# Turning a table lookup's indices with one VectorE transpose in place of TensorE, in an embedding kernel

## The chip, the cores and the metric

One core of one Trainium2 chip. The metric is the device time of one execution in microseconds (us); the median of the runs is quoted. The experiments ran on three chips. The kernel before took 181.7 to 181.8 us on the first (called A here) and 176.1 to 176.2 us on the other two (B and C), so only runs of one chip are compared, or runs of B with runs of C, which agree within 0.1 us.

## The reference

```python
batch, seq_len, vocab_size, d_model = 32, 512, 50000, 512
token_embed = embedding_table[indices]            # indices: [32, 512]
return (token_embed + position_embed).astype(np.float32)   # [32, 512, 512]
```

16,384 rows of 2 KB are fetched, a position row is added to each, and 33.5 MB are written. The indices reach the core as 64-bit words; the low half of each is used.

## The kernel before

A sequence `b` lies on 128 partitions with 4 positions (`k`) on each. GpSimd issues 128 gathers; each takes one column of 128 indices and fetches 256 KB. VectorE adds the positions out of PSUM, ACT issues all other loads and all stores. For the first four sequences the indices are loaded in the layout that the gathers want, in small packets. The rest are loaded in rows, cast to float, turned by TensorE against an identity and cast back.

```python
with tc.tile_critical(sync_engine=nc.vector.engine, no_gpsimd_drain=True):
    nc.scalar.dma_start(out=idx0[:, 0, :], in_=idx_first[:, 0, :]).then_inc(s_first, 16)
    load_pos(0)                                   # half of the positions, 512 KB
    nc.scalar.dma_start(out=idx0[:, 1:, :], in_=idx_first[:, 1:, :]).then_inc(s_next, 16)
    nc.scalar.dma_start(out=idx_raw[:], in_=...).then_inc(s_raw, 16)      # 128 rows of 1 KB
    nc.scalar.wait_ge(s_pos[0], 16)
    load_pos(1)
    nc.gpsimd.affine_select(out=ident[:], ...)
    nc.gpsimd.wait_ge(s_first, 16)
    for g, (b, k) in enumerate(order):
        if g == half:       nc.gpsimd.wait_ge(s_next, 16)           # half is 2
        if g == FIRST * K:  nc.gpsimd.wait_ge(s_prep, 2 + K + J)    # 16: turned indices
        ...                                       # where = idx0[...] if b < FIRST else idx_t[...]
        nc.gpsimd.indirect_dma_start(out=slots[b % SLOTS][:, k, :], ...)
    # TensorE: 4 transposes; VectorE: 1 cast before them, 4 after, between its adds
    ...
tc.no_sync_barrier()
nc.scalar.wait_ge(s_rest, nc.scalar.to_reg(16 * rest))
```

## Time and profile before

| | before |
|---|---|
| time, median of 3 runs | 181.71 us (181.65 to 181.85) |
| span of the profiled run | 178.1 us |
| GpSimd | 133 instructions, 121.8 us busy |
| VectorE | 137 instructions, 91.4 us busy |
| TensorE | 4 transposes, 1.0 us busy |

Read the GpSimd row with care: 68% busy looks like slack, but each gather also has 0.30 us of "issue" before it, time in which the engine waits for nothing that the profile shows.

### The profile page before, as it was taken

The page shows a single profiled execution, that of the slowest core. Times are in us where ns is not written, and L with a number is a line of the kernel's source. Part 1 is how long each engine was busy: PE and PEld are TensorE (multiplying, and loading weights), DVE is VectorE, ACT ScalarE, POOL GpSimd, SP SyncE. Part 2 cuts the span into 40 slices and gives each one's busy share as a digit, 9 for nine tenths or more (in the row PEclk, how much of TensorE's full clock was granted, in tenths as well). Part 3 has the DMA queues.
Part 4 walks back from the last instruction along what each step waited for, and adds up shares of the span by engine and source line. Part 5 has one row for each costly group of instructions (what it writes and reads, how often), then busy time and mean ns, then how long its engine had stood idle before and what let it go on. Part 6 is the DMA issues. An engine that isn't in the chain of part 4 may idle for free.

```text
span 178.1 us, 415 instructions
## 1 busy us (share of the span) xinstructions
PE 1.0 (1%) x4; PEld 0.4 (0%) x4; DVE 91.4 (51%) x137; POOL 121.8 (68%) x133
## 2 busy tenths in 40 slices
PE   0000100000000000000000000000000000000000
PEld 0000000000000000000000000000000000000000
DVE  0445973455556555555556455555556555554510
POOL 3777777777777777777777777777777777774000
DMA  4899999999999999999999999999999999999960
GB/s 122 234 329 359 375 378 364 385 410 413 416 416 419 419 419 420 419 420 419 419 420 420 419 419 418 419 418 419 420 419 420 418 420 420 420 419 421 417 258 0
DMA packets 21011, 68.34 MB, mean 384 GB/s; under 512 B 3728, under 2 KB 3856, under 8 KB 21008
## 3 DMA queue, kind: packets, MB, share of 16 engines
q10 hardware_dynamic: 10768, 34.76, 48.6%
q0 software_dynamic: 10240, 33.56, 48.1%
q14 instruction: 3, 0.02, 0.0%
HBM read 34.75 MB, written 33.55 MB: 384 GB/s over the span
## 4 chain that ended last, share of the span: by engine, by line
POOL 65%; issue 23%; DMA 5%; DVE 2%; ACTq 0%; DVEq 0%
POOL slot L136 65%; DMA slot<-in_embedding_table_dram,idx_t 4%; DVE slot L171 2%; DMA idx<-in_indices_dram 1%; ACTq L211 0%; DVEq L101 0%
## 5 line engine op out<-in xcount | busy, mean ns | idle before, releaser
L136 POOL DMA_INDIRECT slot<-in_embedding_table_dram,idx_t x112 | 106.0, 946 | 34.1 <-issue 34.1
L171 DVE TENSOR_TENSOR slot<-slot,pos_ps 128x512 f32<-128x512 f32 x128 | 87.7, 687 | 73.8 <-issue 57.8
L136 POOL DMA_INDIRECT slot<-in_embedding_table_dram,idx x16 | 15.3, 958 | 6.0 <-issue 4.6
L166 DVE COPY pos_ps<-pos_sb 128x512 f32<-128x512 f32 x4 | 2.7, 685 | 4.9 <-DMA pos_sb<-in_position_embed_dram 4.9
L162 DVE CAST idx_t<-turned 32x128 int32<-32x128 f32 x4 | 1.1, 280 | 0.1
L149 PE MATMUL turned<-ident,idx_f 128*32 128x128 f32 x4 | 1.0, 413 | 17.6 <-issue 17.6
L118 POOL TENSOR_SCALAR_AFFINE_SELECT ident<-const-float32-1.0 128x128 f32<-128x128 f32 x1 | 0.3, 282 | 0.7 <-DVEq L101 0.7
L149 PEld LDWEIGHTS turned<-ident,idx_f 128*32 128x32 f32 x4 | 0.4, 131 | 17.7 <-issue 17.6
L200 POOL MEMSET const-float32-0.0<- 128x1 f32 x1 | 0.1, 99 | 0.3 <-issue 0.3
L156 DVE CAST idx_f<-idx_raw 128x128 f32<-128x128 int32 x1 | 0.2, 220 | 0.0
L200 POOL MEMSET const-uint8-127<- 128x1 uint8 x1 | 0.1, 116 | 0.0
L200 POOL MEMSET const-bfloat16-1.0<- 128x1 bf16 x1 | 0.1, 110 | 0.0
L200 POOL MEMSET const-float32-1.0<- 128x1 f32 x1 | 0.1, 102 | 0.0
## 6 DMA issues: line engine op xcount, KB each, us to landing
out_dram<-slot ACTq DMA_DIRECT2D x60, 512.0 KB
out_dram<-slot ACTq DMA_DIRECT2D x8, 256.0 KB
slot<-in_embedding_table_dram,idx_t POOLq DMA_INDIRECT x112
pos_sb<-in_position_embed_dram ACTq DMA_DIRECT2D x2, 512.0 KB, 4.7
slot<-in_embedding_table_dram,idx POOLq DMA_INDIRECT x16
idx_raw<-in_indices_dram ACTq DMA_DIRECT2D x1, 128.0 KB
idx<-in_indices_dram ACTq DMA_DIRECT2D x1, 4.0 KB, 1.6
idx<-in_indices_dram ACTq DMA_DIRECT2D x1, 12.0 KB
```

Of the source, the lines that this page charges most:

```text
L118: nc.gpsimd.affine_select(out=ident[:], in_=nc.const_aps.tensor(1.0, [P, P], f32), pattern=[[-1, P]], compare_op=mybir.AluOpType.is_equal, ...
L136: ins = nc.gpsimd.indirect_dma_start(out=slots[b % SLOTS][:, k, :], out_offset=None, in_=table, in_offset=bass.IndirectOffsetOnAxis(ap=whe ...
L149: nc.tensor.transpose(turned[:, k].rearrange("p b j -> p (b j)"), idx_f[:, :, k], ident[:]).then_inc(s_prep, 1)
L156: nc.vector.tensor_copy(out=idx_f[:].rearrange("r p k -> r (p k)"), in_=idx_raw[:, :, 0])._wait_ge(s_raw, 16).then_inc(s_prep, 1)
L162: nc.vector.tensor_copy(out=idx_t[j * Q : (j + 1) * Q, :, :], in_=turned[:, :, :, j]).then_inc(s_prep, 1)
L166: nc.vector.tensor_copy(out=pos_ps[:, k, :], in_=pos_sb[:, k, :])._wait_ge(s_pos[k // half], 16).then_inc(s_ps, 1)
L171: nc.vector.tensor_tensor(out=part, in0=part, in1=pos_ps[:, k, :], op=add)._wait_ge(s_gather[g % LANES], rounds(g)).then_inc(s_add, 1)
L200: nc = _bacc.Bacc("TRN2", target_bir_lowering=False, num_devices=1)
```

## The change

The intent is to take TensorE, the identity, the PSUM tile and five casts out of the index path. The row blocks are loaded with the 32 sequences on each quadrant of 32 partitions, in four loads, and one VectorE transpose of 128x128 words then yields the gathers' layout for all sequences: in this layout that means turning each square of 32x32 words where it lies. The small load for sequences 1 to 3 goes away, so everything from the third gather on waits for the transpose. GpSimd, not VectorE, gives the signal with which the section begins and ends.

```diff
-    with tc.tile_critical(sync_engine=nc.vector.engine, no_gpsimd_drain=True):
+    with tc.tile_critical(sync_engine=nc.gpsimd.engine, no_gpsimd_drain=True):
-        nc.scalar.dma_start(out=idx0[:, 0, :], in_=idx_first[:, 0, :]).then_inc(s_first, 16)
+        nc.scalar.dma_start(out=idx0[:, :], in_=idx_first).then_inc(s_first, 16)
         load_pos(0)
-        nc.scalar.dma_start(out=idx0[:, 1:, :], in_=idx_first[:, 1:, :]).then_inc(s_next, 16)
-        nc.scalar.dma_start(out=idx_raw[:], in_=...).then_inc(s_raw, 16)
+        for j in range(J):                                            # J is 4
+            nc.scalar.dma_start(
+                out=idx_raw[j * B : (j + 1) * B, :], in_=idx_rows[:, j, :]
+            ).then_inc(s_raw, 16)
         nc.scalar.wait_ge(s_pos[0], 16)
         load_pos(1)
-        nc.gpsimd.affine_select(out=ident[:], ...)
...
             if g == half:
-                nc.gpsimd.wait_ge(s_next, 16)
-            if g == FIRST * K:
-                nc.gpsimd.wait_ge(s_prep, 2 + K + J)
+                nc.gpsimd.wait_ge(s_idx, 1)
...
-        for k in range(K): nc.tensor.transpose(turned[:, k]..., idx_f[:, :, k], ident[:])
+        nc.vector.transpose(
+            out=idx_t[:],
+            in_=idx_raw[:].rearrange("r (q k w) -> r k q w", k=K, w=2)[:, :, :, 0],
+        )._wait_ge(s_raw, 16 * J).then_inc(s_idx, 1)
...                                               # (five casts between the adds: gone)
```

More of the change, by code (lines that the diff above doesn't have):

```diff
@@ L38 @@
     assert S == P * K and B == 32
-    assert V < (1 << 24), "an index passes through float32"
     J = P // Q
+    assert B == Q, "indices are turned in squares of 32"
     idx_words = indices.bitcast(i32)
-    idx_first = idx_words[0:FIRST].rearrange("b (p w) -> p b w", p=P)
-    idx_rows = idx_words.rearrange("b (j w) -> (b j) w", j=J)
+    idx_first = idx_words[0].rearrange("(p w) -> p w", p=P)
+    idx_rows = idx_words.rearrange("b (j w) -> b j w", j=J)
     out_rows = out.rearrange("b (p k) d -> b p k d", k=K)
@@ L57, in psum @@
         return ctx.enter_context(pool).tile(shape, dtype, name=name)
-    idx0 = sbuf("idx0", [P, FIRST, 2 * K], i32)
-    idx_raw = sbuf("idx_raw", [P, Q * K, 2], i32)
-    ident = sbuf("ident", [P, P], f32)
-    idx_f = sbuf("idx_f", [P, Q, K], f32)
+    idx0 = sbuf("idx0", [P, 2 * K], i32)
+    idx_raw = sbuf("idx_raw", [P, 2 * Q * K], i32)
     idx_t = sbuf("idx_t", [P, K, B], i32)
@@ L65 @@
     slots = [sbuf(f"slot{n}", [P, K, D], f32) for n in range(SLOTS)]
-    turned = psum("turned", [Q, K, B, J], f32)
     pos_ps = psum("pos_ps", [P, K, D], f32)
@@ L82 @@
     sem = tc.alloc_semaphore
-    s_first, s_next, s_raw = sem("s_first"), sem("s_next"), sem("s_raw")
+    s_first, s_raw, s_idx = sem("s_first"), sem("s_raw"), sem("s_idx")
     s_pos = [sem(f"s_pos{h}") for h in range(2)]
@@ L88 @@
     s_out, s_rest = sem("s_out"), sem("s_rest")
-    s_prep, s_ps, s_add = sem("s_prep"), sem("s_ps"), sem("s_add")
+    s_ps, s_add = sem("s_ps"), sem("s_add")
     def rounds(g):
@@ L99, in load_pos @@
         )
-    with tc.tile_critical(sync_engine=nc.vector.engine, no_gpsimd_drain=True):
-        nc.scalar.dma_start(out=idx0[:, 0, :], in_=idx_first[:, 0, :]).then_inc(
-            s_first, 16
-        )
+    with tc.tile_critical(sync_engine=nc.gpsimd.engine, no_gpsimd_drain=True):
+        nc.scalar.dma_start(out=idx0[:, :], in_=idx_first).then_inc(s_first, 16)
         load_pos(0)
-        nc.scalar.dma_start(out=idx0[:, 1:, :], in_=idx_first[:, 1:, :]).then_inc(
-            s_next, 16
-        )
-        nc.scalar.dma_start(
-            out=idx_raw[:], in_=idx_rows.rearrange("r (s w) -> r s w", w=2)
-        ).then_inc(s_raw, 16)
+        for j in range(J):
+            nc.scalar.dma_start(
+                out=idx_raw[j * B : (j + 1) * B, :], in_=idx_rows[:, j, :]
+            ).then_inc(s_raw, 16)
         nc.scalar.wait_ge(s_pos[0], 16)
         load_pos(1)
-        nc.gpsimd.affine_select(
-            out=ident[:], in_=nc.const_aps.tensor(1.0, [P, P], f32),
-            pattern=[[-1, P]], compare_op=mybir.AluOpType.is_equal, fill=0.0,
-            base=0, channel_multiplier=1,
-        ).then_inc(s_prep, 1)
         nc.gpsimd.wait_ge(s_first, 16)
@@ L131 @@
                 nc.gpsimd.wait_ge(s_out, 16 * done)
-            if b < FIRST:
-                where = idx0[:, b, 2 * k : 2 * k + 1]
+            if g < half:
+                where = idx0[:, 2 * k : 2 * k + 1]
             else:
@@ L144 @@
         nc.gpsimd.drain()
-        nc.tensor.wait_ge(s_prep, 2)
-        for k in range(K):
-            nc.tensor.transpose(
-                turned[:, k].rearrange("p b j -> p (b j)"), idx_f[:, :, k], ident[:]
-            ).then_inc(s_prep, 1)
-        for g, (b, k) in enumerate(order):
-            if g == 7:
-                nc.vector.tensor_copy(
-                    out=idx_f[:].rearrange("r p k -> r (p k)"), in_=idx_raw[:, :, 0]
-                )._wait_ge(s_raw, 16).then_inc(s_prep, 1)
-            if g == 9:
-                nc.vector.wait_ge(s_prep, 2 + K)
-                for j in range(J):
-                    nc.vector.tensor_copy(
-                        out=idx_t[j * Q : (j + 1) * Q, :, :], in_=turned[:, :, :, j]
-                    ).then_inc(s_prep, 1)
+        nc.vector.transpose(
+            out=idx_t[:],
+            in_=idx_raw[:].rearrange("r (q k w) -> r k q w", k=K, w=2)[:, :, :, 0],
+        )._wait_ge(s_raw, 16 * J).then_inc(s_idx, 1)
+        for g, (b, k) in enumerate(order):
             if b == 0:
```

## The prediction

> **What bounds the kernel now.** I read the page from the top down: the 40 slices, the chain that ended last, the groups, then the timeline of the first 25 us and of the end. The slices first:
>
> ```profile
> POOL 3777777777777777777777777777777777774000
> DMA  4899999999999999999999999999999999999960
> GB/s 122 234 329 359 375 378 364 385 410 413 416 416 419 419 419 420 419 420 419 419 420 420 419 419 418 419 418 419 420 419 420 418 420 420 420 419 421 417 258 0
> ```
>
> GpSimd shows an even 7 tenths up to slice 36, and the DMA engines are full. The chain and the groups say why GpSimd's 7 is in truth a full engine:
>
> ```profile
> POOL 65%; issue 23%; DMA 5%; DVE 2%; ACTq 0%; DVEq 0%
> L136 POOL DMA_INDIRECT slot<-in_embedding_table_dram,idx_t x112 | 106.0, 946 | 34.1 <-issue 34.1
> L171 DVE TENSOR_TENSOR slot<-slot,pos_ps 128x512 f32<-128x512 f32 x128 | 87.7, 687 | 73.8 <-issue 57.8
> L162 DVE CAST idx_t<-turned 32x128 int32<-32x128 f32 x4 | 1.1, 280 | 0.1
> L149 PE MATMUL turned<-ident,idx_f 128*32 128x128 f32 x4 | 1.0, 413 | 17.6 <-issue 17.6
> ```
>
> Each of 128 gathers takes 0.95 us of GpSimd and has 0.30 us of issue before it. The idle time is issue and no wait: all 34.1 us before the 112 gathers are "issue". So one gather starts every 1.25 us, and the chain is 88% GpSimd and issue. The last gather starts at 161.94 in the timeline of the end; the first at 2.89; 127 gaps of 1.25 us are 158.9, which with the 0.2 us extra of the first gap gives 159.05. That is the whole span but for a head of 2.89 us and a tail of 178.1 - 161.94 = 16.2 us. The head:
>
> ```profile
> 1.03 0.38 ACTq L104 DMA_DIRECT2D idx<-in_indices_dram  x1
> 1.18 0.28 POOL L118 TENSOR_SCALAR_AFFINE_SELECT ident<-const-float32-1.0 128x128 f32<-128x128 f32 x1 [0.67 <-DVEq L101]
> 1.44 0.45 ACTq L97 DMA_DIRECT2D pos_sb<-in_position_embed_dram  x1
> 1.93 0.46 ACTq L108 DMA_DIRECT2D idx<-in_indices_dram  x1
> 2.41 0.51 ACTq L111 DMA_DIRECT2D idx_raw<-in_indices_dram  x1
> 2.89 1.14 POOL L136 DMA_INDIRECT slot<-in_embedding_table_dram,idx  x1 [1.43 <-DMA idx<-in_indices_dram]
> 4.33 0.95 POOL L136 DMA_INDIRECT slot<-in_embedding_table_dram,idx  x1 [0.31 <-issue]
> 4.93 0.33 ACTq L97 DMA_DIRECT2D pos_sb<-in_position_embed_dram  x1
> 4.93 0.69 DVE L166 COPY pos_ps<-pos_sb 128x512 f32<-128x512 f32 x1 [4.93 <-DMA pos_sb<-in_position_embed_dram]
> 5.59 0.95 POOL L136 DMA_INDIRECT slot<-in_embedding_table_dram,idx  x1 [0.30 <-issue]
> ```
>
> GpSimd's one wait is for the first indices, 1.03 to 2.61. The identity is made inside that wait (1.18 to 1.46), and the third gather starts at 5.59. That moment, 5.59, is the one that the change puts at risk.
>
> Whether the DMA engines are a second bound decides how much a late gather costs. The table by windows gives 417 GB/s from 30 to 150 us at a share of 1.03, and 360 GB/s at a share of 0.99 from 20 to 30 us. So "full" engines moved more later: fullness is no fixed rate. From the timelines, the first gather's add starts 3.8 us after the gather, the ones near 90 us some 7.9 us after, the last 7.65 us after (161.94 to 169.59). A backlog builds in the first 30 us and then stands still for 130 us, with no gather ever waiting for its lane. I read it as engines that follow GpSimd's pace at about 512 KB per 1.25 us, or 419 GB/s, so a shift of the gathers shifts the end.
>
> [...] No transpose on VectorE is in the trace of before; the nearest are the 0.22 us cast of 128x128 and the 0.28 us casts out of PSUM. [...] The transpose reads one word in every 32 bytes; the old cast read one in every 8. So I allow 0.30 to 0.45 us. [...] each issue holds ACT's queue for 0.33 to 0.51 us.
>
> **The change part by part.**
>
> *TensorE, identity, casts gone.* Identity 0.28 us, transposes 1.04 us from first to last, VectorE's five casts 0.22 + 1.21 us and a short wait at 19.9 us. None is on the chain: the identity lies inside GpSimd's 1.43 us wait, the casts lie between adds, and no gather waited for the turned indices (the first to use them starts at 23.09 after the usual 0.30 us). Worth to the end: 0. VectorE gains some 1.5 us between 17 and 21 us, and a few early stores leave sooner; GpSimd doesn't wait for stores there. Also 0.
>
> *GpSimd leads the section.* Before, GpSimd and ACT both wait for VectorE's signal; ACT's first issue is at 1.03. GpSimd is released a little sooner than VectorE, so its signal should come about 0.05 us earlier, and the first index load with it. Gain 0.05 us, estimated from the events at the barrier, which lie some 0.05 us apart.
>
> *One index load fewer, and four in place of one.* ACT's order is now first indices, half the positions, four loads of 32 rows. ACT is free for the first of the four at 1.88 (1.93 less 0.05). An issue costs 0.33 to 0.51 us with 0.03 between; at some 0.40 the four start at 1.88, 2.31, 2.74 and 3.17. The packet records of before have the first packet of a load 1.0 to 1.1 us after the start of its issue where nothing is ahead. So the fourth could move at 4.2 to 4.3. But the positions are ahead in the same queue: their packets run from 2.55 to 4.57, and they land at 4.91. In before the small packets of the second index load (384 of 32 bytes) came next, 4.18 to 4.71, then the raw indices, most at 4.3 to 5.0 and the last at 5.50, landing at 5.84. With the small packets gone I put the last raw packet at 4.6 to 4.8, and the landing some 0.35 us later, 4.95 to 5.15.
>
> *The new wait.* VectorE starts the transpose about 0.02 us after the landing, as it did on the positions (4.91 to 4.93). 5.05 + 0.02 + 0.38 = 5.45, and 0.05 for the signal. GpSimd, when it waits, starts busy work about 0.28 us after a landing (2.61 to 2.89). So gather three starts at 5.50 + 0.28 = 5.78. It was 5.59. Loss 0.19 us, and everything after it follows at 1.25 us.
>
> *VectorE's start.* Its first position copy moves from 4.93 to about 5.45 and ends at 6.14, still before the first gather lands (6.67). Cost 0.
>
> *The tail* is unchanged: the same lag, adds, stores.
>
> Sum: the start of gather three moves by +0.19 with the head gain already in it (ACT's earlier start). 181.71 + 0.19 = 181.90 us.
>
> **The rivals.**
>
> *A: the transpose is ready in time.* If the four issues are cheap (0.33 us) and the raw packets slip in by 4.4, the landing is 4.75, and GpSimd's third gather starts at 5.54, right behind the second. Then the head gain is all that stays: 181.65. [...] against it that all of these loads stand behind the positions.
>
> *B: a long stall takes the place of the spare wait.* If an issue of 32 rows costs the full 0.51 us and the last load trails as one did in before (5.50), landing is 5.85 to 6.1, the transpose ends at 6.3 to 6.6, and gather three starts at 6.6 to 6.9: 1.0 to 1.3 us late, 182.7 to 183.0. For it speaks the straggler in before; against it that its cause may have been the small packets and the first gather's own packets, which start at 4.87.
>
> *C: the DMA engines are the bound.* Then a late third gather is swallowed by the backlog, the 1.5 us sooner on VectorE and the missing small packets count for a little, and the time is 181.4 to 181.7. For it speaks the share of 1.03 and the full slice after the last gather; against it the standing backlog and the change from 360 to 419 GB/s at the same fullness.
>
> **Range and chances.** Centre 181.9. A and C give 181.4 to 181.7, B up to 183. Nothing here reaches 2% (3.6 us) either way: the whole head is 2.89 us, of which 1.58 us is the load of the first indices, which stays. A slowdown of 2% needs gather three at 9.2 us. Range 181.3 to 182.8; faster 0.01, same 0.97, slower 0.02.
>
> **What would show it.** The first index load should start near 0.98, gather one near 2.84, gather two near 4.28. The transpose should be one row of 0.30 to 0.45 us that starts at 5.0 to 5.2 and waits for the raw indices. GpSimd's waits should hold one for VectorE of about 0.2 to 0.6 us on the third gather, then only issue, at 1.25 us. The lag from gather to add should be 7.6 to 8.1 us again from 40 us on: if it is smaller by what GpSimd lost, C is right. I am wrong if the four loads land past 5.5, if the transpose costs over 0.6 us, if the pace of 1.25 us changes, or if the tail after the last gather is not 16.2 us.

## The result, and the profile after

| | before | after |
|---|---|---|
| time, median of 4 runs | 181.68 us (181.65 to 181.85) | 183.08 us (182.96 to 183.17) |
| span of the profiled run | 178.1 us | 179.5 us |
| third gather starts | 5.59 us | 6.83 us |
| last gather starts | 161.94 us | 163.54 us |
| last add starts | 169.59 us | 171.07 us |

The ratio is 1.0075 (95% interval 1.0057 to 1.0092). The change costs 1.40 us: within 2%, but above the predicted range.

The timeline of the first 8 us after the change answers to the head shown in the prediction (rows that bear on nothing here are left out of this and the later timelines; columns: start, duration, engine, line, operation, and in brackets the idle time before it and what ended it):

```profile
0.90 0.38 ACTq L99 DMA_DIRECT2D idx<-in_indices_dram  x1
1.31 0.45 ACTq L93 DMA_DIRECT2D pos_sb<-in_position_embed_dram  x1
1.79 1.87 ACTq L102 DMA_DIRECT2D idx_raw<-in_indices_dram  x4
2.81 1.08 POOL L120 DMA_INDIRECT slot<-in_embedding_table_dram,idx  x1 [2.36 <-DMA idx<-in_indices_dram]
4.20 0.95 POOL L120 DMA_INDIRECT slot<-in_embedding_table_dram,idx  x1 [0.30 <-issue]
4.93 0.35 ACTq L93 DMA_DIRECT2D pos_sb<-in_position_embed_dram  x1
6.16 0.41 DVE L131 STREAM_TRANSPOSE idx_t<-idx_raw 128x128 int32<-128x128 int32 x1 [6.16 <-DMA idx_raw<-in_indices_dram]
6.49 0.67 DVE L137 COPY pos_ps<-pos_sb 128x512 f32<-128x512 f32 x1
6.83 0.95 POOL L120 DMA_INDIRECT slot<-in_embedding_table_dram,idx_t  x1 [1.68 <-DVE idx_t L131]
```

The head is earlier than before, as intended (first load at 0.90, not 1.03). Then GpSimd, which has ended its second gather at 5.15, stands for 1.68 us until the transpose is done. The transpose itself is short, 0.41 us. It starts at 6.16 because that is when the four index loads have landed, 2.5 us after the last of them was issued (1.79 + 1.87 = 3.66). The table of waits of the changed kernel has this as its only new wait of GpSimd (columns: who waited for whom, us in total, times, longest):

```profile
POOL slot L120 <- issue: 38.4, 126, 0.3
DVE idx_t L131 <- DMA idx_raw<-in_indices_dram: 6.2, 1, 6.2
POOL slot L120 <- DMA idx<-in_indices_dram: 2.4, 1, 2.4
POOL slot L120 <- DVE idx_t L131: 1.7, 1, 1.7
```

From there on the gathers follow at 1.25 us each, and the groups show nothing that took longer than before:

```profile
L120 POOL DMA_INDIRECT slot<-in_embedding_table_dram,idx_t x126 | 119.5, 949 | 39.8 <-issue 38.1
L142 DVE TENSOR_TENSOR slot<-slot,pos_ps 128x512 f32<-128x512 f32 x128 | 88.0, 688 | 74.8 <-issue 49.0
L131 DVE STREAM_TRANSPOSE idx_t<-idx_raw 128x128 int32<-128x128 int32 x1 | 0.4, 405 | 6.2 <-DMA idx_raw<-in_indices_dram 6.2
```

A gather takes 949 ns here and 946 in the profile of before, and the median step from gather to gather is 1.254 against 1.251 us. Over 125 steps that is 0.4 us. It need not be an effect of the change: unchanged kernels show 1.254 in some profiles and 1.251 in others (1.254 in both controls on chip A, 1.251 in the one on C).

### The profile page after: what moved, and what is told of

It is laid out like the page before. It is cut to its first block, busy times and chain, and to the rows that moved or that the text cites. A ratio compares the mean times of both kernels' runs of the same rounds, so it can differ in the third digit from the quotient of the medians.

```text
span 179.5 us, 397 instructions
## 1 busy us (share of the span) xinstructions
DVE 90.8 (51%) x133; POOL 121.8 (68%) x132
## 4 chain that ended last, share of the span: by engine, by line
POOL 64%; issue 23%; DMA 6%; DVE 2%; ACTq 1%; POOLq 0%
POOL slot L120 64%; DMA slot<-in_embedding_table_dram,idx_t 4%; DMA idx_raw<-in_indices_dram 2%; DVE slot L142 2%; ACTq L102 1%; ACTq L93 0%; DVE idx_t L131 0%; ACTq L99 0%; POOLq L128 0%; ACTq L182 0%; POOLq L97 0%; POOLq L171 0%
## 5 line engine op out<-in xcount | busy, mean ns | idle before, releaser
L120 POOL DMA_INDIRECT slot<-in_embedding_table_dram,idx_t x126 | 119.5, 949 | 39.8 <-issue 38.1
L120 POOL DMA_INDIRECT slot<-in_embedding_table_dram,idx x2 | 2.0, 1016 | 2.7 <-DMA idx<-in_indices_dram 2.4
```

What stands on the lines that cost most here:

```text
L120: ins = nc.gpsimd.indirect_dma_start(out=slots[b % SLOTS][:, k, :], out_offset=None, in_=table, in_offset=bass.IndirectOffsetOnAxis(ap=whe ...
```

## The experiments

The kernel's last wait, against a register's value: every experiment moves that wait into the end of the section, against a constant:

```diff
+        nc.scalar.wait_ge(s_rest, 16 * rest)
     tc.no_sync_barrier()
-    nc.scalar.wait_ge(s_rest, nc.scalar.to_reg(16 * rest))
```

The kernel before with that edit is "the control", the changed kernel with it "the changed kernel, wait moved". "Over before" is the difference of medians to the unedited kernel before on the same chip, in the same rounds.

### The controls, on chips A, C and A

> A control that only moves the last wait (for the stores that nobody else waits for) from behind the section into its end, because a wait against a register may not be used in these experiments. All theories: same head, same pace of 1.25 us, gather three at 5.6 us; the tail may be longer by up to 0.5 us, so 181.7 to 182.3.

> The control (kernel before, last wait moved) again, so that the next three have it on their own chip; the runs with one fill had none, and their chip's times lay 3% lower. All theories: 0.1 to 0.3% over the kernel before.

> The control on the same chip as the two long fills and the next. 0.1 to 0.3% over the kernel before.

Measured: 182.14 us (+0.39 over before), 176.45 us (+0.26) and 181.88 us (+0.06). So the edit costs 0.1 to 0.4 us, and two runs of one control differ by 0.26 us on chip A: differences below 0.3 us are not read here. On chips B and C the time of a profiled run is its span plus 1.7 to 1.8 us in all six kernels; on chip A the two do not run together so well, which matters below.

### The changed kernel, wait moved, twice on chip A

> The changed kernel with the same move of the last wait. Theory 1 (GpSimd's pace is the bound and the late third gather is the whole loss): 1.2 to 1.6 us over the control, gather three at 6.8 us, raw indices landed near 6.1 us. If the loss came from the end of the section (GpSimd leads it), the difference to the control would change here, to under 0.8 or over 2 us.

> The changed kernel with its last wait moved, again, beside the next three. If the DMA engines' idle time at the start is what a late third gather costs, it is 0.8 to 1.3 us over the kernel before, on whatever chip.

Measured: 183.17 us (+1.42 over before, 1.03 over the control) and 183.05 us (+1.31). The transposes start at 5.80 and 5.95, the third gathers at 6.47 and 6.63. The loss is not made at the end of the section: it is there with another end. The first of these missed its range: 1.2 to 1.6 us over the control had been expected, and the 1.03 fits neither theory's figures. Its landing was earlier than in the first profile; its third gather is 0.78 us behind the control's, which started at 5.69.

### The index loads ahead of the positions, chip A, twice

```diff
-        load_pos(0)
         for j in range(J):
             nc.scalar.dma_start(out=idx_raw[j * B : (j + 1) * B, :], ...)
+        load_pos(0)
```

> The changed kernel with the four index loads issued ahead of the first position load. Theory 1a (the four loads land late because they stand behind the positions in one queue and their last packets meet those of the first gather, from 4.7 us on): the last of the four starts near 2.75 us, they land by 4.4 us, the transpose ends by 4.9 us, gather three follows gather two without a wait near 5.45 us, and the time falls to 0.0 to 0.2 us under the control. Theory 1b (four small loads on one semaphore are slow in themselves, whatever stands beside them): they still land 2.9 us after the last issue, near 5.6 us, gather three near 6.3 us, 0.7 us over the control. The positions land later, near 6.3 us; the first add may start later, but nothing waits for it.

> The changed kernel with the four index loads ahead of the positions, again, beside the control and on the same chip: the candidate that beats both. Gather three without a wait near 5.4 us, indices landed by 4.5 us; 0.1 to 0.5 us under the control. If the lag from gather to add decides the end as much as the start does, it can be within 0.2 us of the control either way.

Measured: 181.80 us (0.34 under the control) and 181.90 us (level with it). The timeline of the first of these:

```profile
1.30 1.87 ACTq L101 DMA_DIRECT2D idx_raw<-in_indices_dram  x4
2.76 1.08 POOL L120 DMA_INDIRECT slot<-in_embedding_table_dram,idx  x1 [2.31 <-DMA idx<-in_indices_dram]
3.20 4.01 ACTq L93 DMA_DIRECT2D pos_sb<-in_position_embed_dram  x2
4.14 0.95 POOL L120 DMA_INDIRECT slot<-in_embedding_table_dram,idx  x1 [0.30 <-issue]
4.47 0.41 DVE L131 STREAM_TRANSPOSE idx_t<-idx_raw 128x128 int32<-128x128 int32 x1 [4.47 <-DMA idx_raw<-in_indices_dram]
5.40 0.95 POOL L120 DMA_INDIRECT slot<-in_embedding_table_dram,idx_t  x1 [0.30 <-issue]
6.86 0.69 DVE L137 COPY pos_ps<-pos_sb 128x512 f32<-128x512 f32 x1 [1.99 <-DMA pos_sb<-in_position_embed_dram]
```

The same four issues of 1.87 us in all now land 1.3 us after the last of them (3.17 to 4.47; 1.4 in the repeat), not 2.1 to 2.5. The third gather follows the second without a wait, at 5.40. The positions are there at 6.86, 1.9 us later than before, and VectorE waits for them, but no gather does. The edit takes back the whole loss, 1.1 to 1.4 us: the wait for the transpose was the loss, and the place of the loads in the order of issue was why it was long. As a candidate to beat the kernel before it is level: 0.34 us in one, nothing in the other.

### No gather while the indices load, chip A

```diff
         nc.gpsimd.wait_ge(s_first, 16)
+        nc.gpsimd.wait_ge(s_raw, 16 * J)
```

> The changed kernel in which gather one also waits until the raw indices have landed, so that no gather packet is in flight while they load. It is slower on purpose. Theory 1a in the form 'the last raw packets wait for the packets of the first gather': the raw indices now land at 4.9 to 5.2 us in place of 6.1. If only the queue behind the positions matters, or the four issues themselves, they land at 6.0 to 6.2 us as before, and gather one starts at 6.4. All: the time is 2 to 3.5 us over the control, since all gathers start later.

Measured: the transpose starts at 5.79, against 5.80 with the gathers running, on the same chip; the time is 185.45 us (one run, +3.70), with the third gather at 9.30. Missed: I had put the late landing down to the first gather's packets, and without them the loads land just as late. In this one run, the gathers' packets are not the cause.

### The index loads in a queue of their own, chip C

```diff
-            nc.scalar.dma_start(out=idx_raw[j * B : (j + 1) * B, :], ...)   # behind load_pos(0)
+            nc.sync.dma_start(out=idx_raw[j * B : (j + 1) * B, :], ...)     # SyncE, first of all
```

> The changed kernel with the four index loads issued from SyncE, in a queue of their own, while ACT issues the first indices and the positions. If the queue behind the positions is what made them late, they land before 4.6 us, gather three does not wait (5.4 us), the positions land near 5.0 us, and the time is 0.1 to 0.5 us under the control, like the run with the loads issued ahead. If the 16 engines themselves were the limit whatever the queue, they land after 5.2 us and gather three waits.

Measured: 177.32 us, +1.13 over before and 0.87 over the control on that chip. The gain I had hoped for is missed; it is the second case of the expectation, a landing after 5.2 and a gather that waits:

```profile
0.90 0.40 ACTq L103 DMA_DIRECT2D idx<-in_indices_dram  x1
1.33 4.41 ACTq L93 DMA_DIRECT2D pos_sb<-in_position_embed_dram  x2
3.16 1.08 POOL L120 DMA_INDIRECT slot<-in_embedding_table_dram,idx  x1 [2.71 <-DMA idx<-in_indices_dram]
5.77 0.41 DVE L131 STREAM_TRANSPOSE idx_t<-idx_raw 128x128 int32<-128x128 int32 x1 [5.77 <-DMA idx_raw<-in_indices_dram]
6.45 0.94 POOL L120 DMA_INDIRECT slot<-in_embedding_table_dram,idx_t  x1 [0.96 <-DVE idx_t L131]
```

SyncE issued its four loads from 0.89 to 2.66, and they still land at 5.77. In the packet records of this trace the first load moves ahead of the positions' packets, and about half of the second moves among them at 3.2 to 3.7. The packets of the last two move from 4.5 to 5.2 us, when most of the positions' packets are through (they end at 4.9 to 5.0), though the last load was issued at 2.24. So a queue of their own did not bring all the loads past the positions; being issued and moving before them did. The first indices are also later here (gather one at 3.16, not 2.81). Why a second queue is held up so is not settled.

### The small index loads put back, chip B

```diff
+        nc.scalar.dma_start(out=idx0[:, 1:, :], in_=idx_first[:, 1:, :]).then_inc(s_next, 16)
         for j in range(J): ...                    # the four loads, and the transpose, stay
             if g == half:
-                nc.gpsimd.wait_ge(s_idx, 1)
+                nc.gpsimd.wait_ge(s_next, 16)
+            if g == FIRST * K:
+                nc.gpsimd.wait_ge(s_idx, 1)
```

> The changed kernel with one part undone: the first four sequences take their indices from the small loads again, as before, and only gather 17 and later take the transposed ones. TensorE, identity and casts stay gone, GpSimd still leads, the four loads and the transpose stay. Theory 1 (the whole loss is the wait of gather three for the transpose): gather three at 5.45 to 5.7 us, no wait for VectorE, time as the control with the moved wait (182.1) or 0.1 less. If the transpose or the four loads cost something in another way (traffic, VectorE later), 182.5 or more. The transpose's start also shows when the indices land with the 384 small packets ahead of them: near 5.8 to 6.2 us if the small packets do not matter, 0.4 us later than in the changed kernel if they do, as the prediction took them to.

Measured: 176.10 us, 0.03 under before (ratio 0.9994, 0.9967 to 1.0022).

```profile
5.57 0.95 POOL L123 DMA_INDIRECT slot<-in_embedding_table_dram,idx  x1 [0.30 <-issue]
6.76 0.41 DVE L134 STREAM_TRANSPOSE idx_t<-idx_raw 128x128 int32<-128x128 int32 x1 [6.76 <-DMA idx_raw<-in_indices_dram]
```

The third gather starts at 5.57 without a wait. Without TensorE, identity and casts, with GpSimd leading and the VectorE transpose in place, the kernel is level with the one before: those parts of the change are worth nothing that this run resolves (the interval runs from 0.6 us faster to 0.4 slower). The transpose starts at 6.76, the latest of all runs, and 0.6 to 1.0 us after the changed kernel's 5.80 to 6.16. That is not all the work of the 384 small packets ahead: with one issue more in front, the last of the four issues also ends 0.53 us later (4.19, not 3.66), and another chip lies between. What is left for the packets is 0.1 to 0.5 us, hardly more than the 0.36 by which the changed kernel's own profiles differ. The run also tells what the split into four costs. One load of 128 rows behind the same small packets landed, by the packet records of four profiles of control-like kernels that hold all 16 landings, at 5.27, 5.52, 5.61 and 5.96. Four loads of 32 rows behind them: 6.74, that is 0.8 to 1.5 us later. The later issue is enough to account for it: the one load's issue ends at 2.85 to 2.92, the last of the four at 4.19. From the end of issue to the landing it takes 2.4 to 3.1 us for the one and 2.5 for the four.

### GpSimd as the leader, alone, chip B

```diff
-    with tc.tile_critical(sync_engine=nc.vector.engine, no_gpsimd_drain=True):
+    with tc.tile_critical(sync_engine=nc.gpsimd.engine, no_gpsimd_drain=True):
```

> The kernel before (last wait moved) with GpSimd in place of VectorE as the engine that leads the section, and nothing else. Theory: first index load and gathers start 0.1 us earlier (0.90 in place of 1.03 us), and so the end: 0.05 to 0.15 us under the control of 182.1. If leading costs GpSimd at the end of the section, it is equal or slower.

Measured: 176.41 us, +0.28 over before, as the control on the sister chip (+0.26). The first load does start earlier, at 0.96 in place of 1.03, but its landing varies by more than that: the first gather starts at 3.06 in this profile. No gain is to be seen in the time, whose interval, half a microsecond either way, would hide one of 0.1.

### Stalls made on purpose: where in the run does a late gather count?

A fill of a tile that nobody reads stands in for a stall on GpSimd, ahead of gather three or ahead of gather 65, 128x1024 (chip B) or 128x3072 (chip A):

```diff
+            if g == 2:                            # or 64
+                nc.gpsimd.memset(scratch[:], 0.0)
```

> The kernel before (last wait moved) with one fill of 128x1024 on GpSimd ahead of gather three, which stands in for the stall. Theory 1 (GpSimd's pace is the bound): the end moves by what the third gather is late, some 0.8 to 2 us by the profile's own reading of the fill. Rival C (the DMA engines are the bound and their backlog swallows the delay): the end moves by under a third of it, and the lag from gather to add in mid-run is smaller by the rest.

> The same fill ahead of gather 65, in the middle of the stream, where the backlog is at its full height. Theory 1: the end moves by the same amount as with the fill ahead of gather three, and the lag from gather to add, smaller just after the fill, is back at its old height by the end. Rival C: the end moves little, under a third of the fill, and the lag stays smaller up to the end.

> One fill of 128x3072 on GpSimd ahead of gather three of the control: it starts some 2.8 us late. Theory 1 (GpSimd's pace is the whole bound): 2.5 to 3.0 us over the control. Rival C (the DMA engines are full and the backlog swallows a stall): at the start there is no backlog yet, so most counts, 1.6 to 2.8 us.

> The same fill ahead of gather 65, with the backlog at its height. Theory 1: 2.5 to 3.0 us over the control, the lag from gather to add back at 7.3 to 8.2 us by the end. Rival C: under 1.0 us over the control, and a lag of 4.5 to 5.5 us from the fill to the end.

> The long fill ahead of gather 65, again, because on the first chip its time (0.25 us over the control) and its span (2 us over) did not agree. If the backlog swallows the stall: 0.2 to 0.8 us over the kernel before in time; on a chip where span and time run together, the span says so too, with the last gather some 2.5 us later than the control's and a lag from gather to add some 2.5 us smaller at the end. If GpSimd's pace is the bound: 2.5 us or more over, and the lag unchanged.

| stall | chip | stall added | time | over before |
|---|---|---|---|---|
| none (controls) | A; C | 0 | 182.14, 181.88; 176.45 | +0.39, +0.06; +0.26 |
| gather three, short | B | 0.83 us | 177.23 | +1.10 |
| gather three, long | A | 2.78 us | 184.68 | +2.86 |
| gather 65, short | B | 0.83 us | 176.58 | +0.45 |
| gather 65, long, twice | A | 2.5 us | 182.13, 182.30 | +0.31, +0.56 |

The stall at the start is the third gather's start less the 5.59 of before; in mid-run it is the longest step between two gathers, 2.08 and 3.78 us, less the usual 1.25. At the start a stall counts in full: +1.10 and +2.86 are the stalls plus the controls' own 0.1 to 0.4 us. That is the case of the changed kernel, and it fits it: 1.24 us of stall, 1.40 us of time. In mid-run a stall hardly counts in the time. The long fills show this clear of the noise; the short ones do not by themselves, since their intervals overlap (0.5 to 1.5 us over before at the start, 0 to 1.2 in mid-run).

For the short one the trace on chip B suggests how. DMA share and GB/s are the last two columns of this view by windows; the fill begins at 82.72, and the gather behind it starts 2.08 us after the one before:

```profile
80.00:84.00 4.00, 0.00 (x0) 0.00 (x0) 2.31 (x4) 3.23 (x5) 1.00 1.03 418
84.00:86.00 2.00, 0.00 (x0) 0.00 (x0) 0.95 (x2) 1.70 (x2) 1.00 1.02 418
86.00:88.00 2.00, 0.00 (x0) 0.00 (x0) 1.37 (x2) 1.39 (x3) 1.00 1.04 422
```

The DMA engines do not notice: 418, 418 and 422 GB/s. They can live on gathers that were issued earlier, since near 90 us an add started some 7.9 us after its gather in the profile of before. The end of the run, first the control on chip C, then the kernel with the mid-run fill:

```profile
161.99 0.95 POOL L136 DMA_INDIRECT slot<-in_embedding_table_dram,idx_t  x1 [0.30 <-issue]
...
169.86 0.69 DVE L171 TENSOR_TENSOR slot<-slot,pos_ps 128x512 f32<-128x512 f32 x1 [0.46 <-DMA slot<-in_embedding_table_dram,idx_t]
```

```profile
162.64 0.95 POOL L139 DMA_INDIRECT slot<-in_embedding_table_dram,idx_t  x1 [0.30 <-issue]
...
169.87 0.69 DVE L174 TENSOR_TENSOR slot<-slot,pos_ps 128x512 f32<-128x512 f32 x1 [0.42 <-DMA slot<-in_embedding_table_dram,idx_t]
```

The last gather starts 0.65 us later, and the last add at the same time: the lag between them has shrunk from 7.87 to 7.23 us, as if the backlog had swallowed the stall. One pair of profiles can't prove it: in the unchanged GpSimd-led kernel on chip B the last add starts at 170.45, and with the short fill at the start it starts at 170.12, with the span no more than 0.1 us over the control's.

For the long fill the records do not agree with each other. In time it is swallowed (+0.31 and +0.56 over before). In the trace it is not: the DMA engines fall to 393 and 373 GB/s from 88 to 98 us, where the control has 420, and the last gather starts at 164.39 and 164.98 against the control's 162.38, with the span 2 us longer, 181.0 and 181.1 against 179.0. The long fill at the start has 181.5: by the spans the two places differ by some 0.5 us, by the times by 2.4 to 2.6. On chip A the time of a profiled run is 1.7 to 4.2 us more than its span for the other kernels, but 0.9 us for these two. Something there lies outside the span that the trace does not show. How much of a long mid-run stall reaches the end stays open.

### The second half of the positions without its wait, chip A

```diff
         load_pos(0)
-        nc.scalar.wait_ge(s_pos[0], 16)
         load_pos(1)
```

> The changed kernel with the index loads ahead of the positions, and without ACT's wait between the two halves of the positions, so that the second half moves at 6 us and not after 8. If the DMA engines are the bound from about 5 us on, filling an idle stretch there brings the end forward: 0.3 to 1.0 us under the version with the wait (which is level with the control). If GpSimd's pace is the bound, no change, within 0.2 us.

> The kernel before (last wait moved) without ACT's wait between the two halves of the positions: the second half moves behind the raw indices at 5 us, where the DMA engines stood idle for 1 us, in place of after 6 us. DMA engines as the bound: 0.3 to 1.0 us under the kernel before's own time plus 0.3. GpSimd's pace as the bound: no change, within 0.2 us.

Measured: 181.92 us (level with 181.90 with the wait) and 182.40 us (0.3 to 0.5 us over the controls). No gain. My premise was wrong as well: I had looked at the packets of ACT's queue alone, and they pause near 5 us, but the view by windows gives the control's engines a share of 0.96 from 5 to 6 us, because the gathers are moving. There was little to fill, so these runs speak for neither bound. They do show that moving the second half of the positions earlier is worth nothing here.

## Why the prediction was wrong

**The step that failed** is "With the small packets gone I put the last raw packet at 4.6 to 4.8, and the landing some 0.35 us later, 4.95 to 5.15." The transpose, which waits for nothing else, started at 6.16, and at 5.80 and 5.95 in the two repeats. Both halves of the step ran over. By the packet records of these three profiles the last index packet ended at 5.53, 5.39 and 5.00, and the landing came 0.60, 0.38 and 0.93 us after it, at 6.13, 5.77 and 5.93: 0.7 to 1.1 us after the 5.05 that the sum used. Rival B's "5.85 to 6.1" came close, but in part by luck: the dearer issue that it named did not come (0.44 us, not 0.51).

The step gave the loads the credit for the small packets that go, and charged nothing for the later issue, because the fourth load "could move at 4.2 to 4.3", before the positions were through. The times of issue that it used were right. What was too small is the time from the end of the last issue to the landing: the prediction left 1.5 us (3.57 to 5.05), and the runs show 2.1 to 2.5. One load of 128 rows behind the same positions took 2.4 to 3.1 in the controls. Only ahead of the positions did the four loads land as fast as that, 1.3 to 1.4 us after the last issue. So the cost that was missing is that of standing behind 512 KB of positions; why it lasts past the positions' own last packet (4.3 to 4.4 us in these profiles) is not shown. The credit for the small packets was too large as well: 0.1 to 0.5 us is what the run with them put back leaves.

The profile of before held the warning: the raw indices landed at 5.84 there. Nobody waited for them until 17 us, so no view by waits shows it, and I read their last packet at 5.50 as a straggler that would go with the small packets. It is a usual landing.

**Most other terms held.** Four issues were put at 1.88, 2.31, 2.74 and 3.17 and ran from 1.79 to 3.66, at 0.44 us each for 32 rows, where the one of 128 rows of the same length took 0.51 in the kernel before. The transpose was put at 0.38, an estimate of mine above the casts of 0.22 and 0.28 us, and took 0.41 (405 ns in all five runs in which its tile was read: `after`, `raw_first`, `hold`, `keep_first` and `raw_sync`); whether reading one word in every 32 bytes has a part in that, no run shows. From its end to the third gather 0.33 us was put, of which the 0.05 for the signal was an estimate of mine, and 0.26 was measured (6.57 to 6.83). Gathers one and two were put at 2.84 and 4.28 and started at 2.81 and 4.20. So of the 1.05 us by which the third gather missed its predicted 5.78, the landing accounts for 1.09: 6.16 against a transpose start of 5.07. One more term went with it: VectorE's first position copy was to end at 6.14, ahead of the first gather's data, and ended at 7.16, so the first add starts at 7.26 in place of 6.68. That costs nothing: it starts later still, at 7.67, in the run with the index loads first, which is level with the control. A slip of no weight is in the sum of the gaps: 127 gaps of 1.25 us are 158.75; the 158.9 takes an unrounded 1.251.

**What was removed is worth nothing**, as predicted, within the half microsecond that the run with the small loads put back can resolve.

**Does the delay reach the end?** Predicted: yes, in full. Shown for the start of the run by the fills there, and by the runs that take the wait away. In the changed kernel itself the lag from the last gather to its add is 7.53 us, against 7.65 before: the backlog did not absorb the delay. The reason given, that the gathers' pace alone sets the end, is not shown: in mid-run most of a stall is missing from the time, as rival C would have it, though the spans don't agree. C was wrong about the third gather.

**The rest of the 1.40 us.** 1.24 us is the third gather. The remaining 0.16 us is no larger than the difference between two runs of one control, and is left unexplained.

**The range** ended at 182.8, inside rival B's own 182.7 to 183.0. A rival with a straggler in the trace behind it had been given less weight than a number that rested on no row.

## What to carry to other kernels

A load whose data nobody is waiting for has a landing time that no wait in the profile shows (the raw indices in the kernel before landed at 5.84 us); before moving its consumer to the front, find that landing in the packet records and take it as it is, rather than argue it down. Small loads that gate a chain belong ahead of the large one in the order of issue; a later place cost 1.1 to 1.4 us here, and a queue of their own did not make up for it. To learn whether a late start counts, put a fill of known length there and, for contrast, in the middle, and make it long enough to stand clear of the noise: 2.8 us at the start cost 2.9 us of time, 2.5 us in mid-run cost 0.3 to 0.6.
